# Two norms behind the output projection of a hybrid decoder layer, laid out tile by tile

## The chip, the cores and the metric

The kernel runs on one core of one Trainium2 chip. The metric is device time in microseconds (us) of one execution. Before the change it is 2803.51 us, the median of three runs from 2800.16 to 2811.13.

## What is computed

One layer of a decoder with 1024 channels, over 2048 prompt positions (with 16 learned ones ahead of them) and 64 sample rows. The token mixer has a stick-breaking attention and a recurrent branch side by side; an output projection and a squared-ReLU MLP follow, each with a norm ahead of it and a norm behind it. The part that matters here:

```python
def rmsnorm(x, g):
    return x * rsqrt(mean(x * x, -1) + 1e-6) * g

def layer(x, ...):
    proj = rmsnorm(x, g_mix_pre) @ w_in
    ...                                    # attention, recurrence
    mixed = concat([attn, lru * gelu(gate)]) @ w_out
    x = x + rmsnorm(mixed, g_mix_post)     # first norm behind the projection
    u = relu(rmsnorm(x, g_mlp_pre) @ w_up) # second norm
    x = x + rmsnorm((u * u) @ w_down, g_mlp_post)
```

## The kernel before

**Tiling.** The prompt is worked in four groups (`s` = 0 to 3) of 512 rows, each of four tiles of 128 rows (`j` = 0 to 3); the last group has the 64 sample rows as a fifth tile (`j` = 4). Every fp32 product is made of three: both operands are split into a high and a low part (`whi`, `wlo` for weights, `ahi`, `alo` and `uh`, `ul` for activations), and TensorE (PE) multiplies high by high, high by low and low by high (L213 to L215, L181 to L183).

**What sets the order.** Only PE runs in the order in which the program is written. The instructions of VectorE (DVE), ScalarE (ACT), GpSimd (POOL) and of SyncE's queue (SP) are ordered by a scheduler before the run, from the order of the program and a model of time; on the chip each of these queues is then fixed. The attention of the next group is cut into small steps that are strewn among the products of the present one. Its steps on DVE are the scan `pb` (L643), the product `beta` (L646) and the low part of the weights of the values `wtl` (L719), which PE needs for `O<-wtl,kv` (L731). The low parts of the MLP's weights, `wlo` (L159), are made on DVE too, in every stage.

**The projection.** `out_proj` (L967) makes the 1024 output channels in two halves, `hf` = 0 and 1, each by `gemm_nat` (L189): the inner dimension in four steps `kp`, within each the tiles in turn, and each tile's sum in one of four PSUM slots (`D`). After `kp` = 3 `evac` empties the tile's slot twice: ACT takes the sum of squares (`mean_sq`, L244) and DVE writes the sum times `g_mix_post` into `y` (L980). The slots are then taken by the next product, `down` of the group before with `hf` = 1, so its first product on a slot waits for that slot's L980.

**The two norms.** When both halves are through, a loop goes over the tiles. For each it takes the root of the first norm (`rstd_of`: a small sum on DVE, L235, and a power on POOL, L237), adds `y * rstd + x` (L994, called *added* here), stores the result to `x1d` (L997), loads the input rows `x` of the tile after the next (L254, two buffers), takes the sum of squares of the added rows on ACT, the root of the second norm (L233, L237), and writes the normed rows (L999, called *normed*). In groups 0 to 2 *normed* writes over the rows that the store reads, so it waits for the store to land. In the last group the sum goes to a buffer of its own (`ahi2`, filled by one load of the group's `x`).

**Who waits for it.** `xpose` (L261) turns the normed rows of all four tiles for the MLP's `up`: PE transposes one 128-column piece of each tile into one PSUM slot `T`, and ACT (L263, `ahi`) and DVE (L264, `alo`) split it. In group 0 `out_proj` stands inside the input projection's last part, and the eight `xpose` follow it. In groups 1 to 3 it stands between the two halves of the last `down` of the group before: `xpose` 0 to 5 are laid between the products of that `down`'s `kp` = 2 and 3, and 6 and 7 at the head of the next `up`. The four places lie at about 725 to 785, 1278 to 1338, 1830 to 1890 and 2325 to 2385 us of the profiled execution.

Of the kernel before, what the change touches and what calls it, by code (L numbers as in the profile page):

```python
# [8 lines left out]
F32 = mybir.dt.float32  # L9
# [4 lines left out]
ALU = mybir.AluOpType  # L14
PSUM = bass.MemoryType.PSUM

P = 128
DM = 1024
# [7 lines left out]
NSAMP = DB * DS  # L26
# [58 lines left out]
def _program(tc, I, O, NSB, NSC):  # L85

    nc = tc.nc
# [4 lines left out]
    def pool(name, side="left", space=None):  # L92
        kw = {"space": space} if space else {}
        cm = tc.tile_pool(name=name, bufs=1, side=side, reuse_waits="tile", **kw)
        p = cm.__enter__()
        pools[side].append((p, cm))
        return p
# [6 lines left out]
    def T(p, shape, dt, tag, bufs=1):  # L104
        uid[0] += 1
        return p.tile(shape, dt, name=f"{tag}_{uid[0]}", tag=tag, bufs=bufs)
# [4 lines left out]
    xp_ = pool("xp")  # L111
    att = pool("att", side="right")

    def psD():
        return T(ps, [P, 512], F32, "D", 4)
# [4 lines left out]
    def psO():  # L120
        return T(ps, [P, 512], F32, "O", 1)
# [40 lines left out]
    def w_next():  # L162
        n = wpos[0]
        wpos[0] += 1
        w_split(n)
        w_load(n + 1)
        w_split(n + 1)
        w_load(n + 2)
        return wsp.pop(n)
# [21 lines left out]
    def gemm_nat(hi, lo, rows, sample, evac, after=None, stagger=False):  # L191

        accs = [psD() if j < 4 else psO() for j in range(rows)]
        sacc = psO() if sample is not None else None
        js = ([rows] if sacc is not None else []) + list(range(rows))
        steps = [([kp], js) for kp in range(4)]
        if stagger:
            steps[2:] = [([2, 3], [j]) for j in js]
        ws = {}
        for kps, jj in steps:  # L200
            for kp in kps:
                if kp not in ws:
                    ws[kp] = [t.rearrange("p (k m) -> p k m", k=2) for t in w_next()]
            for j in jj:
                for kp in kps:
                    whi, wlo = ws[kp]
                    for kk in range(2):
                        k = 2 * kp + kk
                        st, sp = k == 0, k == KC - 1
                        if j < rows:  # L210
                            h, l = hi(k, j), lo(k, j)
                            o = accs[j][0:h.shape[-1]]
                            nc.tensor.matmul(o, h, whi[:, kk, :], start=st, stop=False)  # L213
                            nc.tensor.matmul(o, l, whi[:, kk, :], start=False, stop=False)  # L214
                            nc.tensor.matmul(o, h, wlo[:, kk, :], start=False, stop=sp)  # L215
                        else:
                            h = sample(k)
                            nc.tensor.matmul(sacc, h, whi[:, kk, :], start=st, stop=False)
                            nc.tensor.matmul(sacc, h, wlo[:, kk, :], start=False, stop=sp)
                if 3 in kps:  # L220
                    evac(j, accs[j] if j < rows else sacc)
                if after is not None:
                    after(kps[0], j)
                work.tick(1.28)
# [5 lines left out]
    def rstd_of(parts, rows):  # L230
        ms = T(xp_, [P, 1], F32, "ms", 7)
        if len(parts) == 1:
            nc.vector.tensor_scalar(ms[:rows], parts[0], EPS, None, op0=ALU.add)  # L233
        else:
            nc.vector.scalar_tensor_tensor(ms[:rows], parts[0], EPS, parts[1], op0=ALU.add, op1=ALU.add)  # L235
        r = T(xp_, [P, 1], F32, "rstd", 7)
        nc.gpsimd.tensor_tensor(r[:rows], ms[:rows], nhalf[:rows], op=ALU.pow)  # L237
        return r

    def mean_sq(src, rows):  # L240
        junk = T(xp_, [P, DM], BF16, "junk", 1)
        ss = T(xp_, [P, 1], F32, "ss", 20)
        w = src.shape[-1]
        nc.scalar.activation(junk[:rows, 0:w], src, AF.Square, scale=1.0 / 32.0, accum_out=ss[:rows])  # L244
        return ss[:rows]
# [6 lines left out]
    def x_load(src, rows):  # L252
        t = T(xpool[0], [P, DM], F32, "x", 2)
        nc.sync.dma_start(t[:rows], src)  # L254
        return t
# [661 lines left out]
    class Group:  # L917
# [49 lines left out]

        def out_proj(self):
            hi, lo, sm = self.blocks()
            for hf in range(2):  # L970
                cs = slice(512 * hf, 512 * hf + 512)

                def evac(j, o):
                    rows = self.rows[j]
                    if hf == 0:
                        self.ys[j] = T(xp_, [P, DM], F32, "y", 4) if j < 4 else T(self.px, [NSAMP, DM], F32, "ysm")
                    y = self.ys[j]
                    src = o if j < 4 else self.fold(o)
                    self.parts[j].append(mean_sq(src, rows))
                    nc.vector.tensor_tensor(y[:rows, cs], src, self.gB[0][:rows, cs], op=ALU.mult)  # L980

                gemm_nat(hi, lo, 4, sm, evac)
            js = range(len(self.rows))
            if self.last:
                xa = T(self.pacc, [P, 4, DM], F32, "ahi2")
                nc.sync.dma_start(xa, I["x_prompt"][4 * self.s * P:(4 * self.s + 4) * P, :].rearrange("(j p) d -> p j d", p=P))
                xts = [xa[:, j] for j in range(4)] + [x_load(self.x_in(4), NSAMP)]
            else:
                xts = [x_load(self.x_in(j), P) for j in range(2)]
            for i, j in enumerate(js):  # L990
                rows, y, xt = self.rows[j], self.ys[j], xts[i]
                r = rstd_of(self.parts[j], rows)
                x1 = xt if self.last else y
                nc.vector.scalar_tensor_tensor(x1[:rows], y[:rows], r[:rows], xt[:rows], op0=ALU.mult, op1=ALU.add)  # L994
                if len(xts) < len(js):
                    xts.append(x_load(self.x_in(i + 2), P))
                nc.sync.dma_start(self.x_mid(j), x1[:rows])  # L997
                r = rstd_of([mean_sq(x1[:rows, :], rows)], rows)
                nc.vector.tensor_scalar(y[:rows], x1[:rows], r[:rows], None, op0=ALU.mult)  # L999

        def xpose(self, k):
            xpose_k(self.ys[:4], k, self.K["g_mlp"], self.hi[:, k, :], self.lo[:, k, :])
# [164 lines left out]
    for s in range(NSB):  # L1167
# [5 lines left out]
        for sc in range(NSC):  # L1173
# [14 lines left out]
            if nxt is not None:  # L1188
                def after(kp, j, nxt=nxt):
                    for k in {(2, 2): (0,), (2, 3): (1,), (3, 0): (2,), (3, 1): (3,), (3, 2): (4,), (3, 3): (5,)}.get((kp, j), ()):  # L1190
                        nxt.xpose(k)
# [99 lines left out]
```

## Time and profile before

| | |
|---|---|
| median of three runs | 2803.51 us (2800.16 to 2811.13) |
| profiled execution | 2806.19 us |
| its span in the trace | 2804.3 us |
| mean granted clock of TensorE | 0.986 |
| PE busy | 2698.7 us (96%) |
| DVE busy | 1789.9 us (64%) |
| ACT busy | 1451.3 us (52%) |
| POOL busy | 748.9 us (27%) |

All times of rows are microseconds from the start of the span, in the one profiled execution. "Idle before" an instruction is idle time of its engine, with what ended it behind the arrow: `[4.45 <-DVE y L999]` says that the engine stood still for 4.45 us until an instruction of line 999 on DVE had written `y`. [...] Of DVE, a normed step takes 0.75 us, an added step 1.28, an L980 step 0.68 and a `wlo` step about 1.2.

### The profile page before, as it was taken

To read this page: it belongs to the slowest core of one execution; us is meant where nothing else is said; L and a number is where in the kernel's file an instruction comes from. 1 tells how busy PE (TensorE), PEld (TensorE's weight loads), DVE (VectorE), ACT (ScalarE), POOL (GpSimd) and SP (SyncE) were. 2 spreads that over 40 slices of the span, in tenths; PEclk is the share of its full clock that TensorE was granted. 3 is DMA by queue.
4 is the path that set the end of the run, shared out by engine and by line. 5 is a ranking of instruction groups with operands and counts; after the bars stand their busy time and mean duration, and the time that the engine had idled before them with its cause. 6 is when DMAs were issued, how large, how long until landed. Compare 5 with 4: busy or idle time off the path is not lost.

```text
span 2804.3 us, 38592 instructions
## 1 busy us (share of the span) xinstructions
PE 2698.7 (96%) x13932; PEld 2216.3 (79%) x13932; DVE 1789.9 (64%) x2412; ACT 1451.3 (52%) x2426; POOL 748.9 (27%) x1447
## 2 busy tenths in 40 slices
PE   8999987998899999999999999999999999999998
PEld 7886756776688888887888888878888887998996
DVE  6455364776776777788867777787676436333434
ACT  6466364675665655566555555565555234332332
POOL 5336372442332322233222222442221002000002
PEclk9999998999999999999999999999999999999999
DMA  5465845567534443345543333454333334222223
GB/s 169 133 205 189 267 138 163 145 174 209 166 95 123 119 116 108 107 132 153 154 116 108 107 108 107 129 167 136 103 96 103 113 121 143 96 82 78 82 83 113
DMA packets 177471, 368.39 MB, mean 131 GB/s; under 512 B 49169, under 2 KB 79505, under 8 KB 177281
## 3 DMA queue, kind: packets, MB, share of 16 engines
q1 hardware_dynamic: 103936, 287.41, 32.4%
q0 software_dynamic: 73344, 78.52, 11.3%
q8 instruction: 110, 1.80, 0.3%
q14 instruction: 81, 0.66, 0.1%
HBM read 305.58 MB, written 60.04 MB: 130 GB/s over the span
## 4 chain that ended last, share of the span: by engine, by line
PE 78%; DVE 7%; DMA 5%; POOL 4%; issue 3%; ACT 3%; SPq 0%; DVEq 0%; POOLq 0%; ACTq 0%
PE D L181 11%; PE D L182 10%; PE D L183 10%; PE D L213 10%; PE D L214 10%; PE D L215 10%; PE T L707 4%; PE T L696 4%; PE O L729 2%; PE O L731 2%; DVE pb L643 1%; DMA vd<-vst 1%; DVE wlo L159 1%; POOL rstd L237 1%; DMA q<-qd 1%
## 5 line engine op out<-in xcount | busy, mean ns | idle before, releaser
L159 DVE TENSOR_TENSOR wlo<-wraw,whi 128x1024 fp32r<-128x1024 f32 x368 | 466.1, 1267 | 495.4 <-ACT whi L158 490.0
L181 PE MATMUL D<-ahi,whi 128*128 128x512 f32 (+3 forms) x1920 | 711.8, 371 | 0.7 <-ACT ahi L1012 0.7
L183 PE MATMUL D<-ahi,wlo 128*128 128x512 f32 (+3 forms) x1920 | 686.0, 357 | 2.5 <-DVE wlo L159 2.5
L182 PE MATMUL D<-alo,whi 128*128 128x512 f32 (+3 forms) x1920 | 686.3, 357 | 1.6 <-DVE alo L1013 1.6
L158 ACT CAST whi<-wraw 128x1024 fp32r<-128x1024 f32 x368 | 386.3, 1050 | 477.8 <-PE D L214 285.3
L213 PE MATMUL D<-whi,uh 128*128 128x512 f32 x1024 | 418.6, 409 | 0.0
L183 PEld LDWEIGHTS D<-ahi,wlo 128*128 128x128 f32 x1920 | 364.3, 190 | 54.3 <-DVE wlo L159 3.9
L181 PEld LDWEIGHTS D<-ahi,whi 128*128 128x128 f32 x1920 | 365.2, 190 | 52.8 <-issue 9.1
L214 PE MATMUL D<-whi,ul 128*128 128x512 f32 x1024 | 404.3, 395 | 0.0
L215 PE MATMUL D<-wlo,uh 128*128 128x512 f32 x1024 | 403.9, 394 | 0.0
L182 PEld LDWEIGHTS D<-alo,whi 128*128 128x128 f32 x1920 | 365.5, 190 | 44.3 <-DVE alo L1013 1.8
L634 ACT ACTIVATE keep<-T,nbias 128x512 f32<-128x512 f32 (+6 forms) x352 | 209.9, 596 | 254.2 <-PE T L696 148.2
L643 DVE TENSOR_TENSOR_SCAN pb<-keep,carry 128x512 f32<-128x512 f32 (+1 forms) x228 | 267.7, 1174 | 70.8 <-ACT keep L634 67.6
L645 POOL COPY carry<-pb 128x1 f32<-128x1 f32 x360 | 93.5, 260 | 569.0 <-DVE pb L643 560.5
L719 DVE TENSOR_TENSOR wtl<-T,wth 128x512 fp32r<-128x512 f32 (+1 forms) x320 | 190.6, 602 | 75.2 <-ACT wth L718 74.5
L718 ACT CAST wth<-T 128x512 fp32r<-128x512 f32 (+1 forms) x320 | 166.1, 523 | 122.0 <-PE T L707 118.8
L215 PEld LDWEIGHTS D<-wlo,uh 128*128 128x128 f32 x1024 | 192.2, 188 | 46.7
L646 DVE TENSOR_TENSOR beta<-beta,pb 128x512 f32<-128x512 f32 (+7 forms) x360 | 209.1, 581 | 31.0 <-POOL carry L645 1.5
L213 PEld LDWEIGHTS D<-whi,uh 128*128 128x128 f32 x1024 | 192.7, 188 | 39.4 <-DVE uf L1028 0.5
L214 PEld LDWEIGHTS D<-whi,ul 128*128 128x128 f32 x1024 | 192.9, 188 | 38.3
L635 ACT ACTIVATE beta<-T,bias 128x512 f32<-128x512 f32 (+6 forms) x352 | 208.4, 592 | 0.0
L707 PE MATMUL T<-ident,beta 128*128 128x128 f32 (+1 forms) x1216 | 192.4, 275 | 12.5 <-ACT beta L635 8.6
(237 smaller groups left out, 3907.5 us busy)
## 6 DMA issues: line engine op xcount, KB each, us to landing
wraw<-in_w_up SPq DMA_DIRECT2D x128, 512.0 KB, 3.5
wraw<-in_w_down SPq DMA_DIRECT2D x128, 512.0 KB, 3.5
wraw<-in_w_in SPq DMA_DIRECT2D x64, 512.0 KB, 4.0
q<-qd POOLq DMA_DIRECT2D x32, 512.0 KB, 17.0
wraw<-in_w_out SPq DMA_DIRECT2D x32, 512.0 KB, 3.6
kv<-kd POOLq DMA_DIRECT2D x48, 256.0 KB, 3.8
kv<-vd POOLq DMA_DIRECT2D x48, 256.0 KB, 4.5
y<-in_x_prompt SPq DMA_DIRECT2D x16, 512.0 KB, 6.1
```

What stands on the lines that cost most here:

```text
L158: nc.scalar.copy(hi, r)
L159: nc.vector.tensor_tensor(lo, r, hi.bitcast(F32), op=ALU.subtract)
L181: nc.tensor.matmul(o, whi[:, k, :], ahi(k, a, b), start=(k == 0), stop=False)
L182: nc.tensor.matmul(o, whi[:, k, :], alo(k, a, b), start=False, stop=False)
L183: nc.tensor.matmul(o, wlo[:, k, :], ahi(k, a, b), start=False, stop=(k == KC - 1))
L213: nc.tensor.matmul(o, h, whi[:, kk, :], start=st, stop=False)
L214: nc.tensor.matmul(o, l, whi[:, kk, :], start=False, stop=False)
L215: nc.tensor.matmul(o, h, wlo[:, kk, :], start=False, stop=sp)
L634: nc.scalar.activation(keep[:, 0:n], S, AF.Sigmoid, bias=nbias, scale=-0.125)
L643: nc.vector.tensor_tensor_scan(pb[:, 0:n][:, ::-1], kr, kr, init, op0=ALU.mult, op1=ALU.bypass)
L646: nc.vector.tensor_tensor(beta[:, 0:n], beta[:, 0:n], pb[:, 1:n + 1], op=ALU.mult)
L707: nc.tensor.transpose(t[0:kn, i * P:(i + 1) * P], w[:, c0:c0 + kn], ident)
```

## The change

`out_proj` is written anew. The first half stays as it was. In the second half each tile's `evac` calls `follow(n)`, which lays out, in this order: *added* of the tile before (with the fetch of a further `x` and the store), *normed* of the tile before that, the first root of this tile, and the second root of the tile before. After the last tile two more calls of `follow` empty the pipeline. The first two `x` are fetched ahead of the second half's products. In the last group the sample tile goes first. The instructions are the same in number and shape on PE, DVE, ACT and POOL, and PE's order is the same; lines behind `out_proj` stand 26 lower (L1057 is L1083).

```diff
-                gemm_nat(hi, lo, 4, sm, evac)
+            xts, r1, x1s_, r2 = {}, {}, {}, {}
+            order = ([4] if self.last else []) + list(range(4))
+            def fetch():
+                for i, j in enumerate(order):
+                    if j not in xts:
+                        xts[j] = x_load(self.x_in(j), self.rows[j])
+                        return
+            def added(j):
+                rows, y, xt = self.rows[j], self.ys[j], xts[j]
+                x1 = x1s_[j] = xt if self.last else y
+                nc.vector.scalar_tensor_tensor(x1[:rows], y[:rows], r1[j][:rows], xt[:rows], op0=ALU.mult, op1=ALU.add)
+                fetch()
+                nc.sync.dma_start(self.x_mid(j), x1[:rows])
+                return mean_sq(x1[:rows, :], rows)
+            def normed(j):
+                rows = self.rows[j]
+                nc.vector.tensor_scalar(self.ys[j][:rows], x1s_[j][:rows], r2[j][:rows], None, op0=ALU.mult)
+            def evac(hf, j, o):
...
                 self.parts[j].append(mean_sq(src, rows))
                 nc.vector.tensor_tensor(y[:rows, cs], src, self.gB[0][:rows, cs], op=ALU.mult)
+                if hf == 1:
+                    n = order.index(j)
+                    follow(n)
+            def follow(n):
+                m2 = added(order[n - 1]) if 0 < n <= len(order) else None
+                if n > 1:
+                    normed(order[n - 2])
+                if n < len(order):
+                    r1[order[n]] = rstd_of(self.parts[order[n]], self.rows[order[n]])
+                if m2 is not None:
+                    r2[order[n - 1]] = rstd_of([m2], self.rows[order[n - 1]])
+            gemm_nat(hi, lo, 4, sm, lambda j, o: evac(0, j, o))
...
+            fetch()
+            fetch()
+            gemm_nat(hi, lo, 4, sm, lambda j, o: evac(1, j, o))
+            follow(len(order))
+            follow(len(order) + 1)
-            for i, j in enumerate(js):
-                rows, y, xt = self.rows[j], self.ys[j], xts[i]
-                r = rstd_of(self.parts[j], rows)
-                x1 = xt if self.last else y
-                nc.vector.scalar_tensor_tensor(x1[:rows], y[:rows], r[:rows], xt[:rows], op0=ALU.mult, op1=ALU.add)
...
-                nc.sync.dma_start(self.x_mid(j), x1[:rows])
-                r = rstd_of([mean_sq(x1[:rows, :], rows)], rows)
-                nc.vector.tensor_scalar(y[:rows], x1[:rows], r[:rows], None, op0=ALU.mult)
```

The scheduler's orders of DVE, ACT, POOL and SP differ from before at the four places alone. In the new code *added* is L984, *normed* L991 and the emptying of a slot L1002. Three of the places on DVE follow; in group 2 `y_17900`, `y_17925`, `y_17947` and `y_17969` are tiles 0 to 3, and the names end with the tile's number in the same way in the others.

DVE in group 2, before, from the emptying of tile 2's slot:

```order
L980 TENSOR_TENSOR y_17947<-D_17987,g_mix_post_6276 128x512
L643 SCALAR_TENSOR_TENSOR pb_18265<-keep_18264,carry_18138 128x512
L719 TENSOR_TENSOR wtl_18279<-T_18273,wth_18278 128x512
L646 TENSOR_TENSOR beta_18263<-beta_18263,pb_18265 128x512
L980 TENSOR_TENSOR y_17969<-D_17988,g_mix_post_6276 128x512
L159 TENSOR_TENSOR wlo_18361<-wraw_18215,whi_18360 128x1024
L233 TENSOR_SCALAR ms_18307<-ss_18305 128x1
L235 SCALAR_TENSOR_TENSOR ms_18312<-ss_17927,ss_18247 128x1
L719 TENSOR_TENSOR wtl_18377<-T_18372,wth_18376 128x384
L999 TENSOR_SCALAR y_17900<-y_17900,rstd_18309 128x1024
L994 SCALAR_TENSOR_TENSOR y_17925<-y_17925,rstd_18314,x_18294 128x1024
```

DVE in group 2, after, from the added step of tile 2:

```order
L984 SCALAR_TENSOR_TENSOR y_17947<-y_17947,rstd_18293,x_18259 128x1024
L991 TENSOR_SCALAR y_17900<-y_17900,rstd_18271 128x1024
L646 TENSOR_TENSOR beta_18302<-beta_18302,pb_18304 128x512
L719 TENSOR_TENSOR wtl_18318<-T_18312,wth_18317 128x512
L1002 TENSOR_TENSOR y_17969<-D_17992,g_mix_post_6276 128x512
L235 SCALAR_TENSOR_TENSOR ms_18337<-ss_17971,ss_18328 128x1
L233 TENSOR_SCALAR ms_18341<-ss_18334 128x1
L159 TENSOR_TENSOR wlo_18361<-wraw_18219,whi_18360 128x1024
L991 TENSOR_SCALAR y_17925<-y_17925,rstd_18297 128x1024
L984 SCALAR_TENSOR_TENSOR y_17969<-y_17969,rstd_18339,x_18284 128x1024
L991 TENSOR_SCALAR y_17947<-y_17947,rstd_18343 128x1024
L719 TENSOR_TENSOR wtl_18377<-T_18372,wth_18376 128x384
```

The `wtl` of 512 columns now stands behind added 2 and normed 0, and the `wtl` of 384 columns behind the emptying of tile 3's slot, a `wlo`, normed 1, added 3 and normed 2; before, only scans, slots and a `wlo` stood ahead of them.

DVE in group 1, before, from the emptying of tile 2's slot (`y_12382`; tile 0 is `y_12360`, tile 3 `y_12402`):

```order
L980 TENSOR_TENSOR y_12382<-D_12431,g_mix_post_6276 128x512
L159 TENSOR_TENSOR wlo_12814<-wraw_12680,whi_12813 128x1024
L980 TENSOR_TENSOR y_12402<-D_12432,g_mix_post_6276 128x512
L233 TENSOR_SCALAR ms_12760<-ss_12758 128x1
L235 SCALAR_TENSOR_TENSOR ms_12765<-ss_12373,ss_12699 128x1
L643 SCALAR_TENSOR_TENSOR pb_12830<-keep_12829,carry_12624 128x512
L994 SCALAR_TENSOR_TENSOR y_12371<-y_12371,rstd_12767,x_12747 128x1024
L999 TENSOR_SCALAR y_12360<-y_12360,rstd_12762 128x1024
```

DVE in group 1, after, the same stretch:

```order
L1002 TENSOR_TENSOR y_12382<-D_12435,g_mix_post_6276 128x512
L235 SCALAR_TENSOR_TENSOR ms_12766<-ss_12384,ss_12755 128x1
L159 TENSOR_TENSOR wlo_12814<-wraw_12684,whi_12813 128x1024
L991 TENSOR_SCALAR y_12360<-y_12360,rstd_12723 128x1024
L233 TENSOR_SCALAR ms_12770<-ss_12763 128x1
L984 SCALAR_TENSOR_TENSOR y_12382<-y_12382,rstd_12768,x_12711 128x1024
L1002 TENSOR_TENSOR y_12402<-D_12436,g_mix_post_6276 128x512
```

Tile 3's slot was emptied one `wlo` behind tile 2's; now normed 0 and added 2 stand between them too.

DVE in group 3, before, from the emptying of tile 1's slot (`y_22459`; tile 0 is `y_22448`, tile 2 `y_22470`, tile 3 `y_22481`, the samples `ysm_22434`):

```order
L980 TENSOR_TENSOR y_22459<-D_22487,g_mix_post_6276 128x512
L994 SCALAR_TENSOR_TENSOR ahi_5344_22650<-y_22448,rstd_22656,ahi_5344_22650 128x1024
L980 TENSOR_TENSOR y_22470<-D_22488,g_mix_post_6276 128x512
L159 TENSOR_TENSOR wlo_22729<-wraw_22597,whi_22728 128x1024
L980 TENSOR_TENSOR y_22481<-D_22489,g_mix_post_6276 128x512
L233 TENSOR_SCALAR ms_22663<-ss_22661 128x1
L235 SCALAR_TENSOR_TENSOR ms_22668<-ss_22461,ss_22627 128x1
L999 TENSOR_SCALAR y_22448<-ahi_5344_22650,rstd_22665 128x1024
L994 SCALAR_TENSOR_TENSOR ahi_5344_22650<-y_22459,rstd_22670,ahi_5344_22650 128x1024
```

DVE in group 3, after, from the `wlo` ahead of it to the emptying of tile 3's slot:

```order
L159 TENSOR_TENSOR wlo_22729<-wraw_22601,whi_22728 128x1024
L1002 TENSOR_TENSOR y_22459<-D_22491,g_mix_post_6276 128x512
L991 TENSOR_SCALAR ysm_22434<-x_22488,rstd_22639 64x1024
L235 SCALAR_TENSOR_TENSOR ms_22657<-ss_22461,ss_22648 128x1
L233 TENSOR_SCALAR ms_22661<-ss_22654 128x1
L1002 TENSOR_TENSOR y_22470<-D_22492,g_mix_post_6276 128x512
L984 SCALAR_TENSOR_TENSOR ahi_5316_22486<-y_22459,rstd_22659,ahi_5316_22486 128x1024
L991 TENSOR_SCALAR y_22448<-ahi_5316_22486,rstd_22663 128x1024
L235 SCALAR_TENSOR_TENSOR ms_22681<-ss_22472,ss_22672 128x1
L984 SCALAR_TENSOR_TENSOR ahi_5316_22486<-y_22470,rstd_22683,ahi_5316_22486 128x1024
L233 TENSOR_SCALAR ms_22685<-ss_22678 128x1
L1002 TENSOR_TENSOR y_22481<-D_22493,g_mix_post_6276 128x512
```

Before, the four slots were emptied with one added step and one `wlo` among them; now the norm steps of the samples and of tiles 0 to 2 stand between the slots' emptyings, and added 0 and that `wlo` ahead of tile 1's.

## Rows read from the trace of the kernel before

**Rows 1.** the page: busy us, share, instructions by engine; the chain that ended last
```profile
PE 2698.7 (96%) x13932; PEld 2216.3 (79%) x13932; DVE 1789.9 (64%) x2412; ACT 1451.3 (52%) x2426; POOL 748.9 (27%) x1447
...
PE 78%; DVE 7%; DMA 5%; POOL 4%; issue 3%; ACT 3%; SPq 0%; DVEq 0%; POOLq 0%; ACTq 0%
```

**Rows 2.** PE's idle time before L261, by releaser (us, times)
```profile
  DVE y L999: 18.1, 10
  DVE alo L264: 13.8, 14
```

**Rows 3.** PE's timeline, group 0: start, duration, instruction, count, idle before and releaser
```profile
756.65 0.63 PE L696 MATMUL T<-kv,q 128*128 128x400 f32 x2 [4.12 <-ACT beta L635]
...
764.87 0.48 PE L261 MATMUL T<-ident,y 128*128 128x128 f32 x1 [4.45 <-DVE y L999]
```

**Rows 4.** stretches, group 0: length; busy PE, PEld, DVE, ACT, POOL; clock; DMA share
```profile
736.00:766.00 30.00, 19.45 (x96) 14.72 (x94) 24.23 (x40) 18.66 (x37) 14.89 (x28) 0.86 0.78 238
760.00:765.00 5.00, 0.55 (x3) 0.26 (x3) 4.99 (x8) 2.13 (x5) 3.85 (x5) 0.50 0.91 296
```

**Rows 5.** timeline of DVE, group 1
```profile
1289.27 1.21 DVE L643 TENSOR_TENSOR_SCAN pb<-keep 128x512 f32<-128x512 f32 x1
...
1294.50 0.68 DVE L980 TENSOR_TENSOR y<-D,g_mix_post 128x512 f32<-128x512 f32 x1
...
1299.24 0.75 DVE L999 TENSOR_SCALAR y<-y,rstd 128x1024 f32<-128x1024 f32 x1 [0.55 <-DMA x1d<-y]
```

**Rows 6.** timeline of PE, group 1
```profile
1296.44 0.39 PE L213 MATMUL D<-whi,uh 128*128 128x512 f32 x1
...
1301.38 0.50 PE L731 MATMUL O<-wtl,kv 128*128 128x512 f32 x1 [0.40 <-DVE wtl L719]
...
1317.80 0.66 PE L261 MATMUL T<-ident,y 128*128 128x128 f32 x4 [1.02 <-DVE alo L264]
```

**Rows 7.** timeline of DVE, group 2
```profile
1840.60 1.27 DVE L994 SCALAR_TENSOR_TENSOR y<-y,rstd,x 128x1024 f32<-128x1024 f32 x1
...
1846.63 0.55 DVE L719 TENSOR_TENSOR wtl<-T,wth 128x384 fp32r<-128x384 f32 x1
```

**Rows 8.** DMA issues, group 2: count, size, median us to landing
```profile
x1d<-y SPq DMA_DIRECT2D x4, 512.0 KB, 4.6
...
x<-in_x_prompt SPq DMA_DIRECT2D x2, 512.0 KB, 4.3
```

**Rows 9.** timeline of PE, group 2
```profile
1847.24 0.44 PE L731 MATMUL O<-wtl,kv 128*128 128x384 f32 x1
...
1849.96 0.39 PE L731 MATMUL O<-wtl,kv 128*128 128x256 f32 x1 [0.33 <-DVE wtl L719]
...
1883.99 0.97 PE L696 MATMUL T<-kv,q 128*128 128x400 f32 x2 [2.48 <-DVE alo L264]
```

**Rows 10.** timeline of DVE, group 3
```profile
2337.72 0.68 DVE L980 TENSOR_TENSOR ysm<-fold,g_mix_post 64x512 f32<-64x512 f32 x1
...
2342.43 1.22 DVE L159 TENSOR_TENSOR wlo<-wraw,whi 128x1024 fp32r<-128x1024 f32 x1
...
2362.58 0.74 DVE L264 SCALAR_TENSOR_TENSOR alo<-T,gT,ahi 128x512 fp32r<-128x512 f32 x1
```

**Rows 11.** timeline of PE, group 3
```profile
2342.76 0.40 PE L213 MATMUL D<-whi,uh 128*128 128x512 f32 x1
...
2345.55 0.40 PE L213 MATMUL D<-whi,uh 128*128 128x512 f32 x1
...
2358.48 0.33 PE L261 MATMUL T<-ident,y 128*128 128x128 f32 x1 [1.23 <-DVE y L999]
...
2378.63 0.40 PE L182 MATMUL D<-alo,whi 128*128 128x288 f32 x1 [1.63 <-DVE alo L1013]
```

**Rows 12.** line L237: durations (min/median/max ns); and one on POOL's timeline
```profile
L237 POOL TENSOR_TENSOR rstd<-ms,nhalf x69: 537/552/2069, 4.7 to 2798.9; 128x1 f32<-128x1 f32 x64, 64x1 f32<-64x1 f32 x4, 16x1 f32<-16x1 f32 x1
...
1862.04 2.07 POOL L237 TENSOR_TENSOR rstd<-ms,nhalf 128x1 f32<-128x1 f32 x1 [0.48 <-DVE ms L233]
```

More of the change, by code (lines that the diff above doesn't have):

```diff
@@ L969, in out_proj @@
             hi, lo, sm = self.blocks()
-            for hf in range(2):
-                cs = slice(512 * hf, 512 * hf + 512)
[L973 to L980, printed above, removed]
-                gemm_nat(hi, lo, 4, sm, evac)
@@ L983, in out_proj @@
-            js = range(len(self.rows))
+            xts, r1, x1s_, r2 = {}, {}, {}, {}
[12 more added lines that the diff above has]
+                return mean_sq(x1[:rows, :], rows)
@@ new lines, in normed @@
+            def normed(j):
+                rows = self.rows[j]
+                nc.vector.tensor_scalar(self.ys[j][:rows], x1s_[j][:rows], r2[j][:rows], None, op0=ALU.mult)
+            def evac(hf, j, o):
+                rows = self.rows[j]
+                cs = slice(512 * hf, 512 * hf + 512)
+                if hf == 0:
+                    self.ys[j] = T(xp_, [P, DM], F32, "y", 4) if j < 4 else T(self.px, [NSAMP, DM], F32, "ysm")
+                y = self.ys[j]
+                src = o if j < 4 else self.fold(o)
+                self.parts[j].append(mean_sq(src, rows))
+                nc.vector.tensor_tensor(y[:rows, cs], src, self.gB[0][:rows, cs], op=ALU.mult)
+                if hf == 1:
+                    n = order.index(j)
+                    follow(n)
@@ L986, in out_proj @@
                 nc.sync.dma_start(xa, I["x_prompt"][4 * self.s * P:(4 * self.s + 4) * P, :].rearrange("(j p) d -> p j d", p=P))
-                xts = [xa[:, j] for j in range(4)] + [x_load(self.x_in(4), NSAMP)]
-            else:
-                xts = [x_load(self.x_in(j), P) for j in range(2)]
-            for i, j in enumerate(js):
-                rows, y, xt = self.rows[j], self.ys[j], xts[i]
-                r = rstd_of(self.parts[j], rows)
-                x1 = xt if self.last else y
-                nc.vector.scalar_tensor_tensor(x1[:rows], y[:rows], r[:rows], xt[:rows], op0=ALU.mult, op1=ALU.add)
-                if len(xts) < len(js):
-                    xts.append(x_load(self.x_in(i + 2), P))
-                nc.sync.dma_start(self.x_mid(j), x1[:rows])
-                r = rstd_of([mean_sq(x1[:rows, :], rows)], rows)
-                nc.vector.tensor_scalar(y[:rows], x1[:rows], r[:rows], None, op0=ALU.mult)
+                xts.update({j: xa[:, j] for j in range(4)})
+            fetch()
[3 more added lines that the diff above has]
+            follow(len(order) + 1)
         def xpose(self, k):
```

## Prediction

> **What bounds the kernel now.** I read the page's busy times first: PE works in 96% of the span and fills 78% of the chain that ended last; DVE, the next, is busy in 64% [rows 1]. So nothing is won but PE's idle time, 105.6 us in all (2804.3 - 2698.7). The second view is the line of the transposes, L261, since they alone read the normed rows: before them PE stood still for 18.1 us until a normed step was through and for 13.8 us until an `alo` step was, over all four groups and both norms that end in a transpose [rows 2]. That is the most the change can aim at. The third views are the timelines of PE and DVE at the four places, one place at a time, because they differ: in group 0 PE starves and falls to half its clock [rows 3, 4], in groups 1 and 2 it works almost without a break beside the attention [rows 6, 9], in group 3 there is no attention and PE has one queue of products [rows 11].
>
> **What the change does to the path.** It removes and adds no instruction. It moves *added* and *normed* forward on DVE, and whatever stood ahead of them goes behind: the emptyings of the PSUM slots that the next product takes, and the `wtl` steps that PE wants for the attention. A normed step in groups 0 to 2 waits for its store to land, an added step for its `x` and its root; DVE's queue waits with it. So each place has a gain (the last normed step is sooner) and a price (a slot or a `wtl` is later). I replay each place with the durations of before: *added* 1.27 [rows 7], *normed* 0.75 and slot 0.68 [rows 5], `wlo` 1.22 [rows 10], root 0.55 [rows 12].
>
> Group 0. PE waits 4.45 us for the normed step of tile 3, which is the end of the loop, after 4.12 us for the attention [rows 3]. In the new order that normed step could end about 5 us sooner. But DVE is the limit: it works 4.99 of the 5 us before PE resumes, and of the 30 us around it stands still for 5.77 (30 - 24.23) [rows 4]. The steps that are passed over (attention scans, a `wlo`) must then be done before PE can go on. Of the 5.77 us idle some part is the wait for stores and loads, which at a DMA share of 0.91 [rows 4] stays. I take a gain of 1.5 us; the bounds are 4.5 (the whole wait of rows 3 goes) and a loss of 1 (one passed-over scan, 1.21 [rows 5], becomes the last).
>
> Group 1. Tile 3's slot was emptied at 1295.18 (1294.50 + 0.68) [rows 5], and PE began its product on it at 1296.44 without a wait [rows 6]. Now normed 0 and added 2 stand ahead. Normed 0 began at 1299.24, when the store landed [rows 5]; added 0 now comes ahead of the scan of 1.21 us that it followed, and the store is issued that much sooner or, if `x` no longer stands ahead of it on SP, a little more, so normed 0 begins between 1296.4 and 1298. Behind it 0.75 + 1.27 + 0.68 = 2.70 us: the slot is free at 1299.1, PE waits 2.7 us (up to 4.3). Against that stand PE's four later waits between 1301.38 and 1317.80, in all 2.45 us, the last for an `alo` [rows 6]: they shrink as PE comes later and DVE has its norm steps behind it. DVE's first `alo` comes, by the replay, 0.7 us sooner, and that is what PE follows from there. Gain 0.7; bounds 2 us either way (2.7 not covered at all is the loss of 2 after 0.7).
>
> Group 2. PE's `O<-wtl,kv` of 384 columns began at 1847.24, behind the `wtl` of 1846.63 [rows 9, 7]. That `wtl` now stands behind normed 2, hence behind the store of tile 2, behind added 2, behind the third `x`, whose buffer is free when added 0 is through. Added 0 ended at 1841.87 [rows 7] and now ends some 1.3 us sooner: 1840.5. Then 0.4 to issue on SP, 4.3 for `x`, 1.27 for added 2, 0.4 to issue, 4.6 for the store [rows 7, 8], which is 1851.5; 0.75 for normed 2 and 0.55 for `wtl` make 1852.8. Without the 1.3 us it is 1854.1. PE is 5.6 to 6.9 us late; I take 6.3. PE's five waits between 1849.96 and 1883.99 sum to 4.5 us, the last 2.48 of it [rows 9], and I let all of them absorb: 1.8 is left. An idle stretch of over 4 us was followed by half the clock in group 0 (0.50 at 760 to 765 [rows 4], behind the 4.12 us of rows 3), where 5 us of products cost 2.5 us more; I take 2.2 here. Loss 4; bounds 1 (no clock lost, a part of the chain hidden) and 8 (half of the waits stay, 2.3, and the clock stays low twice as long).
>
> Group 3. The sample tile now goes first: its emptying ends at 2338.40 [rows 10], then 0.15 sum, 0.55 root, 0.2 between engines, added 1.27: 2340.6. Tile 0's slot 0.68, its sum and root 0.75, added 0 1.27, `wlo` 1.22, tile 1's slot 0.68 make 2345.2, where PE wants that slot at 2342.76 [rows 11]: 2.4 us. On to tile 3: normed 0.75, slot 0.68, added 1.27 (+0.2), normed 0.75, root 0.6, added 1.27, slot 0.68 make 2351.4, where PE, 2.4 late, wants it at 2347.95 (2345.55 + 2.4): 3.4 more. PE is 5.8 us late. Its five waits from 2358.48 (1.23 for the last normed step) to 2378.63 (1.63) sum to 5.8 [rows 11], and would cover it whole, were DVE and ACT not late as well: the first `alo`, at 2362.58 before [rows 10], comes at about 2364. Loss 1; bounds a gain of 2 and a loss of 4 (a third of the waits not covered).
>
> **Sum.** -1.5 - 0.7 + 4 + 1 = +2.8 us. On the profiled execution, 2806.19 (span 2804.3 and 1.9 around it), that is 2809.0; it lies 2.7 above the median of the three, so beside the median I predict 2806.
>
> **The rivals.** (a) *The waits cover the prices.* The same mechanism at its good bounds: 4.5 + 2 + 2 gained, 1 lost, in all 7.5 less, 2796. For it: the idle time of rows 6, 9 and 11 is close to the new stalls. Against it: DVE is without idle time at the end of each place. (b) *The slots and `wtl` are in time, and all waits of rows 2 go:* 31.9 us less, 2772. It would need the x1d stores of before to be the only cause; the page's PE row leaves the room, but L261's idle time is in part the queue of DVE itself. Faster by over 0.5% begins at 2789.5. (c) *The roots on POOL are stretched*, which ends slower. A root takes 0.55 us at the median, but up to 2.07, as at 1862.04 [rows 12]. Before, DVE stood idle during many roots; now it goes on with *added*, a slot or a `wlo` while POOL works. Each root that is stretched costs 1.5 us (2.07 - 0.55), and three at each place lie ahead of tile 3's slot: 12 times 1.5 is 18 us, 2824. It decides from 8 of the 12 on (2817.5 is 0.5% above). Against it: many roots of before already lie beside such steps, and the median is 0.55.
>
> [...]
>
> **How the numbers follow.** My forecast, a price that is mostly covered (2803 to 2812): 0.55. (a), 2796: 0.28. (c), 2824: 0.08. (b), 2772: 0.05; the remaining 0.04 is a clock lost at several places, beyond 2818. The runs differ by some 0.4% on their own and a measurement can tell about 0.5% from no change. The range takes in (a) and the sum of the upper bounds, 1 + 2 + 8 + 4 = +15 us: 2796 to 2818; what it leaves out is (b), (c) and the lost clock, 0.17. Faster by over 0.5% 0.06, within 0.5% 0.85, slower 0.09.
>
> **What would show it.** Right: PE waits for DVE L1002 at about 1296.4 and 1299 (group 1) and at 2342.8 and 2348 (group 3), for DVE `wtl` at about 1847 to 1853 (group 2); the wait of 4.45 for the last normed step in group 0 goes, and that stretch still ends with `alo` waits; PE's busy time is the same within a few us. Wrong: no such waits on slots (then the emptyings were not in the way, (a) or (b)), roots of 1.5 us and more in a row at one place (c), or a difference that lies outside the four places.

## The result, and the profile after

The changed kernel takes 2817.01 us at the median of 11 runs (2812.34 to 2823.81), against 2806.13 of 11 runs of before. The ratio is 1.0034, with a 95% interval of 1.0021 to 1.0047: 9.5 us slower by the ratio, 10.9 by the medians, within 0.5%. The profiled execution took 2812.93 us, its span is 2810.9, 6.6 us above that of before. It is one of the fastest of the 11 runs, while that of before lies at the median: the traces explain these 6.6 us, and what the other 3 to 4 us are no trace shows.

PE's waits, before and after, tell most of it. Views: the waits of the PE engine over the whole span (who waits, for whom: us in all, times, longest). Before:

```profile
PE T L261 <- DVE y L999: 8.3, 5, 4.5
...
PE T L261 <- DVE alo L264: 5.7, 7, 1.6
...
PE O L731 <- DVE wtl L719: 0.7, 2, 0.4
```

After, the page's busy times first, then the waits of the same engine:

```profile
PE 2702.4 (96%) x13932; PEld 2218.7 (79%) x13932; DVE 1790.3 (64%) x2412; ACT 1451.4 (52%) x2426; POOL 757.8 (27%) x1447
```

```profile
PE D L213 <- DVE y L1002: 8.8, 3, 5.3
PE O L731 <- DVE wtl L719: 6.8, 3, 3.7
...
PE O L729 <- POOL carry L645: 2.9, 1, 2.9
...
PE T L261 <- DVE alo L264: 1.9, 3, 1.2
```

The waits of the transposes for a normed step are gone, 8.3 us to none, and those for `alo` fell from 5.7 to 1.9. In their place stand 8.8 us for slots (three waits: groups 1 and 3) and 6.8 for `wtl` (almost all in group 2). PE's busy time rose as well, by 3.7 us with the same instructions: in group 1, where the granted clock is 0.50 from 1297 to 1303, products of 512 columns take 0.63 us, and 0.39 from 1305 to 1310, where it is 1.00.

PE carries out the same instructions in the same order in both kernels. So the start of one instruction can be compared between two traces, and the lag of the second followed through the program. Its change from the entry to the exit of a place (725 to 785, 1278 to 1360, 1830 to 1900 and 2335 to 2400 us of the trace of before) is what the place cost, and it is made up of what PE's idle time and PE's busy time rose by over the same instructions:

| us later than before (less is faster) | group 0 | group 1 | group 2 | group 3 |
|---|---|---|---|---|
| forecast, with its bounds | -1.5 (-4.5 to 1) | -0.7 (-2 to 2) | 4 (1 to 8) | 1 (-2 to 4) |
| the changed kernel | -3.1 | 3.8 | 5.4 | 0.5 |
| of it idle time of PE | -3.7 | 1.0 | 4.7 | 0.7 |
| of it busy time of PE | 0.6 | 2.7 | 0.7 | -0.2 |

So what is left of group 1's loss at its exit stands mostly in slower products, and of group 2's in waits. Between the places the lag hardly moves: it is -3.28 us from 785 to 1278. One trace of a place is not exact, though: in the experiments below, places whose code is that of before differ from it by -0.3 to 0.6 (group 0), -0.6 to 1.1, -1.3 to 1.8 and -1.5 to 0.

**Group 1.** Views: DVE's timeline of the changed kernel, then PE's, then SP's (the store of tile 0), then the stretches around (length, busy time of PE, PEld, DVE, ACT, POOL, then the granted clock, the DMA share and GB/s). It answers to [rows 5, 6].

```profile
1291.66 1.22 DVE L159 TENSOR_TENSOR wlo<-wraw,whi 128x1024 fp32r<-128x1024 f32 x1
1296.03 0.75 DVE L991 TENSOR_SCALAR y<-y,rstd 128x1024 f32<-128x1024 f32 x1 [3.15 <-DMA x1d<-y]
1296.70 0.14 DVE L233 TENSOR_SCALAR ms<-ss 128x1 f32<-128x1 f32 x1
1296.76 1.27 DVE L984 SCALAR_TENSOR_TENSOR y<-y,rstd,x 128x1024 f32<-128x1024 f32 x1
1297.96 0.68 DVE L1002 TENSOR_TENSOR y<-D,g_mix_post 128x512 f32<-128x512 f32 x1
```

```profile
1298.69 0.80 PE L213 MATMUL D<-whi,uh 128*128 128x512 f32 x1 [5.30 <-DVE y L1002]
```

```profile
1287.84 0.42 SPq L986 DMA_DIRECT2D x1d<-y  x1
```

```profile
1290.00:1295.00 5.00, 3.39 (x17) 2.35 (x15) 2.88 (x4) 3.59 (x9) 2.58 (x3) 1.00 0.94 329
1295.00:1300.00 5.00, 1.31 (x3) 1.12 (x4) 3.97 (x7) 1.15 (x2) 2.73 (x2) 0.66 0.70 281
1300.00:1305.00 5.00, 5.00 (x18) 3.68 (x18) 3.75 (x6) 2.62 (x4) 2.81 (x5) 0.66 0.81 268
```

Normed 0 stands in DVE's queue 3.15 us until its store has landed; added 2 and the emptying of tile 3's slot stand behind it, and PE waits 5.30 us for that slot. Then the clock is 0.66 on average from 1295 to 1305 (0.50 from 1297 to 1303), and the first product takes 0.80 us where it took 0.39 before [rows 6].

**Group 2.** Views: DVE's timeline (the two `wtl`), PE's, and the stretch between; they answer to [rows 7, 9].

```profile
1849.62 0.68 DVE L719 TENSOR_TENSOR wtl<-T,wth 128x512 fp32r<-128x512 f32 x1
...
1854.76 0.88 DVE L719 TENSOR_TENSOR wtl<-T,wth 128x384 fp32r<-128x384 f32 x2
```

```profile
1850.35 0.80 PE L731 MATMUL O<-wtl,kv 128*128 128x512 f32 x1 [2.94 <-DVE wtl L719]
...
1855.36 0.69 PE L731 MATMUL O<-wtl,kv 128*128 128x384 f32 x1 [3.68 <-DVE wtl L719]
```

```profile
1850.00:1855.00 5.00, 1.33 (x3) 0.75 (x3) 4.93 (x9) 1.31 (x4) 2.20 (x3) 0.50 0.75 266
```

DVE is busy 4.93 of these 5 us, ahead of the second `wtl`; ahead of the first its only idle time is 0.33 us, for a root. No transfer holds it there, it works off the norm steps that stand ahead of the `wtl`.

**Group 3.** PE waits for the slots of tiles 1 and 3, and nowhere for a normed step; this answers to [rows 11].

```profile
2351.13 0.65 PE L213 MATMUL D<-whi,uh 128*128 128x512 f32 x1 [2.13 <-DVE y L1002]
...
2357.15 0.50 PE L213 MATMUL D<-whi,uh 128*128 128x512 f32 x1 [1.41 <-DVE y L1002]
```

**Group 0** gained. Its waits of 4.12 and 4.45 us [rows 3] are now these:

```profile
754.68 0.77 PE L729 MATMUL O<-wth,kv 128*128 128x512 f32 x1 [2.92 <-POOL carry L645]
...
757.40 1.11 PE L261 MATMUL T<-ident,y 128*128 128x128 f32 x4 [0.62 <-ACT beta L635]
...
761.21 1.04 PE L696 MATMUL T<-kv,q 128*128 128x400 f32 x2 [2.69 <-ACT beta L635]
```

The normed rows are there in time, and the attention, which was passed over, is late in their place.

### The profile page after: what moved, and what is told of

The parts are those of the page before. It is cut to its first block, busy times and chain, and to the rows that moved or that the text cites. A ratio compares the mean times of both kernels' runs of the same rounds, so it can differ in the third digit from the quotient of the medians.

```text
span 2810.9 us, 38592 instructions
## 1 busy us (share of the span) xinstructions
PE 2702.4 (96%) x13932; PEld 2218.7 (79%) x13932; DVE 1790.3 (64%) x2412; ACT 1451.4 (52%) x2426; POOL 757.8 (27%) x1447
## 4 chain that ended last, share of the span: by engine, by line
PE 79%; DVE 6%; DMA 5%; POOL 4%; issue 3%; ACT 3%; SPq 0%; DVEq 0%; POOLq 0%; ACTq 0%
PE D L213 11%; PE D L181 11%; PE D L214 11%; PE D L215 11%; PE D L182 10%; PE D L183 10%; PE T L707 4%; PE T L696 4%; PE O L729 2%; PE O L731 2%; DMA md<-keep 1%; DMA vd<-vst 1%; POOL gt L527 1%; DVE pb L643 1%; DMA q<-qd 1%
```

## The experiments

The theory: the loss arises where DVE's order puts the emptyings of slots and the `wtl` steps behind norm steps, in groups 1 and 2, and the gain is group 0's. Rivals: the roots on POOL, stretched beside DVE's steps; transfers that come sooner and collide; the waits as such, or the clock that falls behind them. Their place costs, counted as above (in bold where the place is not as before):

| | ratio to before (95%) | group 0 | group 1 | group 2 | group 3 |
|---|---|---|---|---|---|
| the change | 1.0034 (1.0021 to 1.0047) | **-3.1** | **3.8** | **5.4** | **0.5** |
| e1 | 0.9982 (0.9972 to 0.9992) | **-3.7** | 0.5 | 1.8 | 0.0 |
| e2 | 1.0013 (1.0002 to 1.0024) | 0.6 | **2.9** | -1.3 | -1.5 |
| e3 | 1.0031 (1.0020 to 1.0043) | -0.3 | 1.1 | **5.4** | -1.4 |
| e4 | 0.9999 (0.9986 to 1.0012) | **-2.4** | **0.4** | **1.4** | **-2.1** |
| e5 | one run | **-3.3** | **0.5** | **5.4** | **2.1** |
| e6 | one run | 0.2 | **0.4** | -0.3 | -1.5 |
| e7 | 0.9995 (0.9985 to 1.0005) | **-2.4** | -0.6 | 0.8 | **-0.7** |
| e8 | 1.0011 (1.0001 to 1.0022) | **-2.7** | **1.3** | **4.7** | **0.5** |

### e1 to e3: one group at a time

The new `out_proj` and the old one stand side by side, and the group chooses (here for e1; e2 and e3 name group 1 and group 2):

```diff
+        def out_proj(self):
+            {0: self.out_proj_tiles, 1: self.out_proj_loop, 2: self.out_proj_loop, 3: self.out_proj_loop}[self.s]()
```

e1: 

> Tile by tile in group 0 alone, the loop of before in groups 1 to 3. Theory (what the change costs comes in groups 1 and 2, where the emptyings of the slots and the wtl steps stand behind the norm steps on DVE): about 3 us faster than before (0.999), PE behind the place of group 0 is 3 us ahead of the trace of before and stays so to the end. Rival (the cost comes from the chip's rest of the program, not from the places): no difference to the changed kernel's 1.0034.

Measured: 2801.86 us, 0.9982 (0.9972 to 0.9992), 3.7 us ahead behind group 0. The expected side, and faster than both kernels. The lead did not stay, as was expected: in this trace group 2, whose code is that of before, lost 1.8 us, and PE ended 1.9 us ahead.

e2: 

> Tile by tile in group 1 alone. Theory: PE waits about 5 us for the emptying of tile 3's slot at about 1296 us and is 3 to 4 us late behind the place; 1.001 to 1.0015. Rival (the four places add up only together, by transfers that collide): less than 1 us late.

Measured: 2809.43 us, 1.0013 (1.0002 to 1.0024), 2.9 us late, just under what was expected; PE's timeline has the wait again:

```profile
1301.58 0.79 PE L213 MATMUL D<-whi,uh 128*128 128x512 f32 x1 [5.19 <-DVE y L1005]
```

e3: 

> Tile by tile in group 2 alone. Theory: PE waits for two wtl steps, together 6 to 7 us, between 1846 and 1855 us and is 5 to 6 us late behind the place; about 1.002. Rival: less than 1 us late.

Measured: 2814.3 us, 1.0031 (1.0020 to 1.0043), 5.4 us late; the two waits are those of the changed kernel:

```profile
1851.65 0.80 PE L731 MATMUL O<-wtl,kv 128*128 128x512 f32 x1 [2.92 <-DVE wtl L719]
...
1856.66 0.69 PE L731 MATMUL O<-wtl,kv 128*128 128x384 f32 x1 [3.68 <-DVE wtl L719]
```

Each place does alone what it does in the whole: -1.8, 1.3 and 3.1 thousandths make 2.6, within the interval of the whole. The rival that the places only collide together falls.

### e4: the same pipeline, written behind the last slot

```diff
                 nc.vector.tensor_tensor(y[:rows, cs], src, self.gB[0][:rows, cs], op=ALU.mult)
-                if hf == 1:
-                    n = order.index(j)
-                    follow(n)
...
-            follow(len(order))
-            follow(len(order) + 1)
+            for n in range(len(order) + 2):
+                follow(n)
```

> In all groups the norm steps tile by tile in the pipeline's order, and the early fetch of x, but written behind the last emptying of a slot, not between them. Theory (order on DVE): no waits of PE for a slot or of 2 us and more for a wtl; group 0 about 2 us faster than before, groups 1 and 2 within 1 us of before, group 3 about 2 us faster; 0.998 to 0.999. Rival (the roots on POOL, which lie beside DVE steps here as well, are the cost): groups 1 and 2 lose 3 us and more each as in the changed kernel, 1.002 to 1.003. Rival (transfers that come sooner collide): groups 1 and 2 lose 2 us and more each.

Measured: 2805.14 us, 0.9999 (0.9986 to 1.0012): no difference, where 0.998 to 0.999 was expected. PE waits for no slot any more, and groups 1 and 2 lose 0.4 and 1.4 us instead of 3.8 and 5.4. But two waits for a `wtl` of over 2 us, which I had expected to be gone, are there (PE), and in group 1 a step ahead of it shows why (DVE):

```profile
1301.77 0.50 PE L731 MATMUL O<-wtl,kv 128*128 128x512 f32 x1 [2.74 <-DVE wtl L719]
```

```profile
1296.74 0.75 DVE L994 TENSOR_SCALAR y<-y,rstd 128x1024 f32<-128x1024 f32 x1 [2.18 <-DMA x1d<-y]
```

```profile
1849.08 0.45 PE L731 MATMUL O<-wtl,kv 128*128 128x384 f32 x1 [2.43 <-DVE wtl L719]
```

In group 2 DVE is busy 4.72 of the 5 us from 1847 to 1852; an added and a normed step stand ahead of the `wtl`. So the order is the cause of the greater part, and norm steps ahead of attention work keep a smaller one. The stores are issued later here too, so this run alone does not part DVE's order from the transfers; e5 does. The rival of the roots falls with it: in e4's group 1, POOL's roots are stretched as well, against 0.55 us at the median before [rows 12],

```profile
1291.65 1.46 POOL L237 TENSOR_TENSOR rstd<-ms,nhalf 128x1 f32<-128x1 f32 x1 [1.03 <-DVE ms L235]
1293.44 1.52 POOL L237 TENSOR_TENSOR rstd<-ms,nhalf 128x1 f32<-128x1 f32 x1 [0.33 <-DVE ms L233]
1297.64 1.46 POOL L237 TENSOR_TENSOR rstd<-ms,nhalf 128x1 f32<-128x1 f32 x1 [2.67 <-DVE ms L235]
```

and it loses 0.4 us.

### e5: no normed step waits for a store

```diff
-                nc.sync.dma_start(self.x_mid(j), x1[:rows])
+                if self.last:
+                    nc.sync.dma_start(self.x_mid(j), x1[:rows])
                 return mean_sq(x1[:rows, :], rows)
...
                 nc.vector.tensor_scalar(self.ys[j][:rows], x1s_[j][:rows], r2[j][:rows], None, op0=ALU.mult)
+                if not self.last:
+                    nc.sync.dma_start(self.x_mid(j), self.ys[j][:rows])
```

> The changed kernel, but in groups 0 to 2 a tile's rows are stored to x1d behind its normed step, which so waits for no store. It stores the normed rows where the added ones belong, so its output is not the reference's. Order on DVE in group 1: normed 0 stands ahead of a wlo, added 2 and the emptying of tile 3's slot, as in the changed kernel but for the wlo. If the store's landing is what holds tile 3's slot in group 1 (DVE idle 3.15 us for x1d there): PE's wait for the slot falls from 5.2 or 5.3 us to 2.2 or less. If the third x is late as well (issued 1291.1 in the changed kernel, 4.4 us to land): to about 4 us, with DVE idle for x instead.

Measured, one run: in group 1 the wait for the slot is 2.52 us, nearer to the first number than to the second, and the place costs 0.5 instead of 3.8:

```profile
1297.21 0.50 PE L213 MATMUL D<-whi,uh 128*128 128x512 f32 x1 [2.52 <-DVE y L1008]
```

In group 2 it costs 5.4 as in the changed kernel. So the wait for the store to land is 2.8 of the 5.3 us in group 1, where the rival of the transfers has its part, and nothing in group 2, where DVE's own queue is the cause.

### e6: work for PE in the wait of group 1

```diff
+    zbox.append(T(pmlp, [P, P], F32R, "zz"))
+    nc.gpsimd.memset(zbox[0].bitcast(F32), 0.0)
...
             for j in jj:
+                if fill is not None and (kps[0], j) in fill:
+                    for _ in range(fill[kps[0], j]):
+                        nc.tensor.matmul(accs[j - 1][0:P], zbox[0], ws[kps[0]][0][:, 0, :], start=False, stop=False)
```

> Tile by tile in group 1 alone, as in e2, with 20 products by zeros (4.7 us, added to tile 2's sum, which they leave as it is) written ahead of the product that waits for tile 3's slot, so that PE works in that wait. If the half clock behind the wait is a part of the loss: no stretch at 0.66 or less at 1295 to 1310 us, PE's wait for the slot about 0.5 us, and PE 1.5 to 2.5 us less late behind the place than in e2 (there 2.9 us). If the wait alone is the loss: 2.9 us late as in e2.

Measured, one run, PE's timeline and the stretch, then the same stretch of e2:

```profile
1296.63 4.83 PE L207 MATMUL D<-whi,zz 128*128 128x512 f32 x20
...
1301.79 0.50 PE L216 MATMUL D<-whi,uh 128*128 128x512 f32 x1 [0.34 <-DVE y L1009]
```

```profile
1300.00:1305.00 5.00, 4.66 (x23) 3.40 (x22) 4.99 (x8) 1.15 (x2) 4.54 (x4) 1.00 0.70 253
```

```profile
1300.00:1305.00 5.00, 3.42 (x9) 2.62 (x10) 4.99 (x8) 2.03 (x3) 4.56 (x4) 0.66 0.68 243
```

The product starts at 1301.79, at the same time as in e2 (1301.58), for the slot is no sooner free. But the clock stays at 1.00, and the place costs 0.4 us where it cost 2.9. PE's greatest lag, counted from the entry of the place, is 5.4 us against 7.0 in e2, and behind it the later, shorter waits give back 5.0 against 4.1. So of the 2.5 us, 1.6 are the products at half clock; the rest is no more than one trace of a place can differ by. The later waits give back a lag of either kind: over the six traces with a changed group 1 it is 3.5 to 5.0 us, and 4.0 of 4.5 in e5, where the clock was 0.80 and 0.86 in the two stretches from 1295 to 1305. A place loses what its greatest lag is above that, and the half clock added 1.6 us to that lag in e2 and 2.3 in the changed kernel.

### e7: the gaining pieces together

```diff
+            {0: self.out_proj_tiles, 1: self.out_proj_loop, 2: self.out_proj_loop, 3: self.out_proj_behind}[self.s]()
```

> Tile by tile in group 0 as in e1, the loop of before in groups 1 and 2, the pipeline behind the last slot in group 3 as in e4. Theory: group 0 gives 3 to 3.7 us, group 3 1 to 2 us; about 0.998, faster than both kernels. If group 3 gives nothing over the loop: as e1, 0.9982 within its interval.

Measured: 2805.53 us, 0.9995 (0.9985 to 1.0005). A miss: group 0, with the same order of work on DVE, ACT and POOL as in e1, gave 2.4 us and not 3.7, and group 3 gave 0.7, which places left as they were show too. Its interval and that of e1 overlap; what is shown is that e1 is faster than before, and that group 3's piece adds nothing that can be told from none.

### e8: the changed kernel with its waits filled

Products by zeros as in e6 (20 in group 1), and 28 behind tile 2's products in group 2, ahead of the attention's product:

```diff
+                if fill is not None and (kps[0], j, "end") in fill:
+                    for _ in range(fill[kps[0], j, "end"]):
+                        nc.tensor.matmul(accs[j][0:P], zbox[0], ws[kps[0]][0][:, 0, :], start=False, stop=False)
                 work.tick(1.28)
```

> The changed kernel with products by zeros laid into PE's waits of groups 1 and 2: 20 (4.7 us) ahead of the product that waits for tile 3's slot in group 1, 28 (6.5 us) ahead of the attention product that waits for the wtl of 512 columns in group 2. They add nothing to the sums and stand where PE would wait. If the half clock behind the waits is most of the loss: group 1 within 1 us of before, group 2 about 3 us late instead of 5.4, no stretch below 0.9 there, and 1.001 to 1.002 against the 1.0034 of the changed kernel. If the loss in group 2 is the wait alone (two waits of 2.9 and 3.7 us, of which later waits give back 4): group 2 5 us late or more, 1.0025 and more.

Measured: 2810.22 us, 1.0011 (1.0001 to 1.0022), against 1.0034 of the changed kernel; the two intervals just touch. Group 1 costs 1.3 us instead of 3.8, where 1 or less was expected; its greatest lag is 5.3 us instead of 7.8. In group 2 PE's waits and the stretch are

```profile
1844.03 6.70 PE L229 MATMUL D<-whi,zz 128*128 128x512 f32 x28
...
1852.37 0.44 PE L738 MATMUL O<-wtl,kv 128*128 128x384 f32 x1 [0.88 <-DVE wtl L726]
```

```profile
1850.00:1855.00 5.00, 4.12 (x24) 3.29 (x23) 2.90 (x6) 2.43 (x5) 0.78 (x2) 1.00 0.84 266
```

with the clock at 1.00 there, but the place costs 4.7 us, and 3 was expected. PE's greatest lag fell by 1.8 us (from 9.3 to 7.5, both counted from the entry); behind it 2.8 were given back instead of 3.8. The zeros end after the first `wtl` is written, but PE still waits 0.88 us for the next one, so they do not set the end. That `wtl` comes no sooner than in the changed kernel: PE's product by it starts at 1852.37 against 1855.36, and PE entered the place 3.0 us sooner. So in group 2 the clock is the lesser part, and most of the loss is that DVE is late with the attention. How much of the rest is which of its steps was not tried.

## Why the prediction was right, and where it was not

The forecast, a small loss within 0.5%, 2806 us in a range of 2796 to 2818, holds the 2817.0 near its upper end. Its mechanism is the one that the traces and e1 to e5 show: a price at slots and at `wtl`, a gain at the last normed step. The sum, 2.8 us, was too small: 6.6 in the profiled pair, some 10 by the runs. That the range holds it is in part luck. 2817.0 lies above the 2803 to 2812 that the forecast gave itself, and is inside only because the range went to the sum of all upper bounds; 2.6 of the 11 us between 2806 and 2817.0 are the base, 2803.5 by three runs and 2806.1 by eleven. The clock lost at several places, which had the remaining 0.04, did come, in groups 1, 2 and 3 (0.66 from 1300 to 1305, 0.50 from 1850 to 1855 and 0.66 from 2350 to 2355), though short of 2818. By its own steps:

- **Group 0**, -1.5: -3.1, and -2.4 to -3.7 over five traces of such a group 0. Inside its bounds; that the attention takes the place of the normed step as the last to come is what the rows show.
- **Group 1**, -0.7, bounds of 2: 3.8 and 2.9. This is the step that failed, in three terms. First, it let normed 0 begin 1.2 to 2.8 us sooner, since its store is issued sooner. The store was issued at 1287.84 and normed 0 began at 1296.03. In the time of before (3.28 later) that is 1291.12 and 1299.31, against 1292.06 and 1299.24 [rows 5]: issued 0.9 us sooner, landed no sooner, and the wait was 5.3 and not 2.7 us. From 1290 to 1295, while it is under way, the DMA engines are busy to 0.94; over the store of before they were busy to 0.52 and 0.73 (the first two rows below); that the store waits among the other transfers is argued from that and not tried. Second, the step had no term for the clock, which group 2's had: behind the wait the lag grows from 5.5 to 7.8 us by products at half clock (0.50 from 1297 to 1303). Third, the gain of 0.7 rested on DVE's first `alo`, which PE was to follow from there. That `alo` came at 1317.45 (the third row, of the changed kernel; 1317.00 before), 3.7 us later when counted from the entry, and DVE had stood idle for ACT's `ahi`: it was DVE that waited. The later waits did cover, 3.4 us by the fourth of them against the 2.45 that I allowed.

```profile
1290.00:1295.00 5.00, 5.00 (x25) 4.09 (x24) 5.00 (x7) 4.50 (x10) 1.95 (x2) 1.00 0.52 132
1295.00:1300.00 5.00, 5.00 (x25) 3.96 (x24) 3.56 (x7) 1.96 (x5) 2.18 (x3) 1.00 0.73 247
```

```profile
1317.45 0.75 DVE L264 SCALAR_TENSOR_TENSOR alo<-T,gT,ahi 128x512 fp32r<-128x512 f32 x1 [1.14 <-ACT ahi L263]
```

- **Group 2**, 4: 5.4, in the changed kernel, e3 and e5. The delay of PE's product, 6.3, came as two waits of 2.94 and 3.68, together 6.6 (7.5 with the products at half clock between them). But the chain by which it was worked out (third `x`, added 2, store of tile 2, normed 2) is not the one that held: DVE's only idle time there was 0.33 us, for a root, and e5, without the wait for the store, loses the same 5.4. The number was right by steps that happen to take as long. The clock, taken at 2.2 from a stretch in which PE worked only 0.55 of 5 us [rows 4], is 1.8 at the greatest lag (e8). Of the 4.5 us of waits that were to absorb, the last, 2.48, stayed (2.5 again); 3.8 us were given back all the same, 1.5 of them because products from 1884 on, which had run at half clock before (0.50 from 1885 to 1887, 0.63 us each), now ran at the full one (1.00 from 1885 to 1895, 0.39 us each).
- **Group 3**, 1: 0.5. The stalls of 2.4 and 3.4 were 2.13 and 1.41, with a stretch at 0.66 of the clock between them (2350 to 2355); PE was 5.6 us late at the most (5.8 forecast), and what came behind covered all but 0.5 of it: the later waits, and 1.2 us by products that had run at half clock before (from 2379.7 on; 0.50 from 2380 to 2382, 0.44 us each, where they take 0.30 in the changed kernel). That 5.6 is so near to 5.8 is luck: 3.5 of it are the stalls, most of the rest is products at half clock (0.50 from 2352 to 2354, 0.63 us each), for which the step had no term.
- **Rival (b)** was built on a wrong bound. The 18.1 and 13.8 us of [rows 2] count a wait twice, once for the weight load's queue (PEld, 9.7 and 8.2) and once for the products (PE); the waits of PE alone were 8.3 and 5.7, so (b) could give at most 14.0 us and not 31.9. They did go, to none and to 1.9, 12.1 us less, and did not bring the time down by that.
- **Rival (c)**, the roots. They are stretched: 8 of the 16 in the changed kernel's groups 1 and 2 take 1.4 to 1.8 us, against 0.55 at the median before [rows 12]. The one of 1.52 us at 1296.9 begins beside the added step of 1296.76; what stretches it is not shown. But DVE waited for the roots less than before (3.9 us ahead of the added steps, 6.0 before), and e4, with roots of 1.5 us, loses 0.4 in group 1. They are not the cause.

## What to carry to other kernels

On an engine with one queue in order, a step that may wait (DVE stood still 3.15 us for a store, 1.88 for a load and 0.33 for a root in the changed kernel), or that merely takes long (DVE was busy 4.93 of 5 us ahead of the second `wtl` of group 2), should not stand ahead of a step for which the bounding engine waits: PE's waits there were 5.30 us in group 1 and 2.94 and 3.68 in group 2. Emptying an accumulator first and pipelining behind it took all 8.8 us of PE's slot waits away again (e4), though it made the kernel no faster than before (0.9999). Laying steps between others pays where the bounding engine stands still anyway, as in group 0 (0.9982 by that group alone, e1), and costs where it is full, as in groups 1 and 2 (1.0013 and 1.0031 by each alone, e2 and e3). Before a wait is priced, look at the clock of the engine behind it: here later waits gave back some 4 us at a place, and products at half clock behind the wait of group 1 added 1.6 us (e2) and 2.3 us (the changed kernel) to what they had to cover.

## What the runs showed of the hardware that I had not expected

- Twenty products by zeros into an open sum, in a wait of 5 us, kept TensorE's granted clock at 1.00 from 1300 to 1305 us, where it was 0.66 in e2's kernel without them. The place cost 2.5 us less, 1.6 of it at the greatest lag (e2 and e6, one trace each). The products that come first behind the wait take 0.79 us without and 0.50 with them.
- A store of 512 KB that was issued 0.9 us sooner landed at the same time (the step behind it began 8.2 us after the issue against 7.2). The DMA engines were busy to 0.94 over five of these 8.2 us, and to 0.52 and 0.73 over the store of before. The issue before, on SP's timeline:

```profile
1292.06 0.42 SPq L997 DMA_DIRECT2D x1d<-y  x1
```
